# A hybrid decoder layer on one core: four gates of the pooling branch's merge are issued before the state-space tables

## Chip, cores and metric

The kernel runs on one core of a Trainium2 chip. The metric is the device time of one execution in microseconds. Three runs of the kernel before took 1079.84 to 1083.04 us, with a median of 1080.96 us. The engines are named as in the profile: PE (TensorE matmul), PEld (its weight loads), DVE (VectorE), ACT (ScalarE), POOL (GpSimd), SP (SyncE, which issues most DMAs).

## The reference, cut to what matters

The input is 512 tokens of 1024 channels in float32. A token mixer has three branches (sparse attention, pooling, state-space), and a sigmoid gate per channel and branch weighs what each branch sends up to 1024 channels:

```
proj = x @ w_in                       # q, k/v, gates, u_pool, u_ssm, bg in its columns
o_pool = pool_mixer(u_pool)           # 512 x 512
o_ssm = ssm_mixer(u_ssm)              # state-space scan, GELU, GLU
gates = sigmoid(bg)                   # 512 x 3 x 1024
merged = gates[0]*(o_nsa @ w_up_nsa) + gates[1]*(o_pool @ w_up_pool) + gates[2]*(o_ssm @ w_up_ssm)
x = layer_norm(ALPHA*x + merged @ w_out)
```

Then comes a mixture of experts (32 experts, two of them per token) and a second layer norm. The state-space branch has complex diagonal states; it runs as tables of powers, small products within blocks of 8 tokens, and a scan over 64 blocks.

## The kernel before, in words

Everything is kept with channels on the partitions and the 512 tokens along the free dimension. To come near float32 with the faster operand type, each operand is split into a high and a low part, and `mm3` (L68 to L72) makes each product as three matmuls: high by high (L70), low by high (L71), high by low (L72). `proj_fm` projects 128 output channels: `whl` splits the weights (cast on ACT, L113, and a subtraction on POOL, L102, into one of 3 buffers "H"), then 8 x 3 = 24 matmuls of 512 columns run into one of 3 PSUM banks "mm".

`merge` (from L762) works through 8 chunks of 128 channels. For a chunk it makes a gate: such a projection, then `tanh` on ACT (L772) into a tile `th`. Then it makes the up projection of 4 x 3 = 12 matmuls from the branch's output (`oph`/`opl` here) and multiplies both on DVE into `mg` (L780). The first call is the pooling branch's.

Ahead of it, `run` issues in this order: `ssm_u` (the state-space inputs U, L564 to L580), `pool_branch` (window products L746 to L750 with `Bf`, `Bm`, `Bn`; split into `pl`, L278 on ACT and L279 on DVE; a product with the group weights in `ps_o`; output split, L757 on ACT and L758 on DVE), the rotations and tables of the first half of the state-space branch (`ssm_rotations`, `ssm_tables(0)`: long DVE work on `T`, `CA` and `Bs`, then L517 on PE, the transposes L547 and their copies `Bc`), and `ssm_half` for both halves. A half makes X on PE (L601), rotates it on DVE (L606 to L611), scans (L614), rotates back (L322 to L327), makes the output on PE (a block of L633 and L635), and applies GELU quarter by quarter (L639 to L645, into `zz`). After the merge, `ssm_z` transposes `zz` (L654) and splits it into `onh`/`onl` (L659, L660), and `ssm_glu` multiplies by its weights: 48 products.

The order is not written out by hand. A scheduler takes the instructions as they are issued, with priorities, and fixes one sequence for each engine; an engine then works strictly in that sequence and waits where an operand isn't there. Rotations and the first tables are issued with raised priority:

```
        with tc.high_priority(offset=HP):
            self.ssm_rotations()
            tabs = self.ssm_tables(0)
        self.ssm_half(0, U[0], tabs)
        tabs = self.ssm_tables(1)
        self.ssm_half(1, U[1], tabs)
        ...
        for _ in self.merge(1, "w_up_pool", self.oph, self.opl, True):
            pass
```

So in the kernel before, the merge's 288 products have the lowest standing of this stretch, and the scheduler puts them where PE would wait for the state-space work.

Of the kernel before, what the change touches and what calls it, by code (L numbers as in the profile page):

```python
# [8 lines left out]
F32 = mybir.dt.float32  # L9
# [4 lines left out]
AF = mybir.ActivationFunctionType  # L14
# [4 lines left out]
S = 512  # L19
D = 1024  # L20
# [13 lines left out]
C_Q, C_KC, C_VC, C_KS, C_VS, C_KW, C_VW, C_NG, C_POOL, C_SSM, C_BG = (  # L34
    0, 512, 640, 768, 896, 1024, 1152, 1280, 1304, 1816, 2328)
# [8 lines left out]
class Build:  # L44
# [714 lines left out]
                                           op0=OP.mult, op1=OP.subtract)  # L759


    def merge(self, b, wname, oh, ol, first, eng="pool"):  # L762
        nc = self.nc
        p = self.mp
        for dc in range(KD):
            if dc % 4 == 0:
                up = self.load_cols(self.I[wname], D, dc * 128, 512, nk=4)
            if dc % 2 == 0:
                w = self.load_cols(self.I["w_in"], 5400, C_BG + b * D + dc * 128, 256)
            ps = self.proj_fm(w, dc % 2, eng)  # L770
            th = p.tile([128, S], F32, name="th", bufs=2)
            nc.scalar.activation(th, ps, AF.Tanh, scale=0.5)  # L772
            if dc % 2 == 0:
                h, l = self.whl(up[:, :, (dc % 4) * 128:(dc % 4 + 2) * 128], 4, 256, eng=eng)
            js = slice(dc % 2 * 128, dc % 2 * 128 + 128)
            pu = self.bank("mm")
            for k in range(4):
                self.mm3(pu, (h[:, k, js], l[:, k, js]), (oh[:, k], ol[:, k]), k == 0, k == 3)
            if first:
                nc.vector.scalar_tensor_tensor(self.kk(self.mg, dc), th, 1.0, pu, op0=OP.add, op1=OP.mult)  # L780
            else:
                nc.vector.scalar_tensor_tensor(th, th, 1.0, pu, op0=OP.add, op1=OP.mult)
                nc.gpsimd.tensor_tensor(self.kk(self.mg, dc), self.kk(self.mg, dc), th, OP.add)
            yield
# [873 lines left out]
    def run(self):  # L1658
        tc, nc = self.tc, self.nc
# [33 lines left out]
        self.oph, self.opl = pair("P", "oph", "opl")  # L1693
        self.pool_branch(pb)
        spb.close()
        with tc.high_priority(offset=HP):
            self.ssm_rotations()
            tabs = self.ssm_tables(0)
# [3 lines left out]
        self.attn_consts(ggp)  # L1702
        self.mg = (self.slab3("G", "mg", 4), self.slab3("Y", "mg", 4))
        self.mg = [t.bitcast(F32) for t in self.mg]
        for _ in self.merge(1, "w_up_pool", self.oph, self.opl, True):
            pass
        sst.close()
        ssp.close()
        son, onp = self.pool("on")
# [85 lines left out]
```

## Time and profile before

| | |
|---|---|
| runs | 1079.84, 1080.96, 1083.04 us |
| the profiled execution's own time | 1077.99 us |
| its span, first to last instruction | 1076.2 us |
| mean granted clock of TensorE | 0.968 |
| PE busy | 984.6 us (91%), 6189 instructions |
| DVE busy | 600.4 us (56%) |
| ACT busy | 320.2 us (30%) |
| POOL busy | 204.1 us (19%) |

In 40 slices of the span (26.9 us each) the granted clock reads 9985999..., so the third and the fourth slice have a lower one; DMA is busy at 99% in nearly all slices from the 24th on, which is the mixture of experts. A timeline row gives the start and the duration in us, then the engine, the line, the operation and its tiles, and in brackets the engine's idle time before it and what ended it. Matmul durations overlap: the distance from one start to the next is what a matmul costs.

### The profile page before, as it was taken

The page shows a single profiled execution, that of the slowest core. Times are in us where ns is not written, and L with a number is a line of the kernel's source. Part 1 is how long each engine was busy: PE and PEld are TensorE (multiplying, and loading weights), DVE is VectorE, ACT ScalarE, POOL GpSimd, SP SyncE. Part 2 cuts the span into 40 slices and gives each one's busy share as a digit, 9 for nine tenths or more (in the row PEclk, how much of TensorE's full clock was granted, in tenths as well). Part 3 has the DMA queues.
Part 4 walks back from the last instruction along what each step waited for, and adds up shares of the span by engine and source line. Part 5 has one row for each costly group of instructions (what it writes and reads, how often), then busy time and mean ns, then how long its engine had stood idle before and what let it go on. Part 6 is the DMA issues. An engine that isn't in the chain of part 4 may idle for free. (4 is left out here: it accounts for less than half of the span.)

```text
span 1076.2 us, 15925 instructions
## 1 busy us (share of the span) xinstructions
PE 984.6 (91%) x6189; PEld 693.6 (64%) x6189; DVE 600.4 (56%) x1437; ACT 320.2 (30%) x669; POOL 204.1 (19%) x183
## 2 busy tenths in 40 slices
PE   7978988999999999999998999999981999999984
PEld 6966666778777787888885566655541555555542
DVE  7992676474788885244455674444442144444456
ACT  4331222344556665233221211111110211111132
POOL 5520313343202222543322000000000000000004
PEclk9985999999999999999999999999995999999997
DMA  6800451315110202924716999999998999999992
GB/s 194 241 1 8 82 114 46 114 43 177 59 40 1 79 2 69 322 84 170 262 70 254 406 419 417 419 418 418 419 418 343 420 418 418 418 418 418 420 402 83
DMA packets 79566, 256.23 MB, mean 238 GB/s; under 512 B 16544, under 2 KB 43712, under 8 KB 54912
## 3 DMA queue, kind: packets, MB, share of 16 engines
q1 hardware_dynamic: 68064, 245.56, 58.4%
q10 hardware_dynamic: 8368, 2.54, 1.9%
q0 software_dynamic: 3056, 7.08, 1.8%
q8 instruction: 50, 0.82, 0.3%
q14 instruction: 28, 0.23, 0.1%
HBM read 254.40 MB, written 4.69 MB: 241 GB/s over the span
## 5 line engine op out<-in xcount | busy, mean ns | idle before, releaser
L1365 PE MATMUL ps_mm<-w,xq 128*64 128x256 f32 x1296 | 148.8, 381 | 1.7 <-DMA w<-in_moe_w_gate_dram 1.6
L102 POOL TENSOR_TENSOR whl<-w,whl 128x1024 fp32r<-128x1024 f32 (+3 forms) x41 | 95.1, 2328 | 274.4 <-ACT whl L113 236.4
L1365 PEld LDWEIGHTS ps_mm<-w,xq 128*64 128x64 f32 x1296 | 92.7, 137 | 56.5 <-issue 11.7
L70 PE MATMUL ps_mm<-xh,whl 128*128 128x512 f32 x288 | 114.9, 399 | 0.0
L72 PE MATMUL ps_mm<-xh,whl 128*128 128x512 f32 x288 | 114.9, 399 | 0.0
L71 PE MATMUL ps_mm<-xl,whl 128*128 128x512 f32 x288 | 114.3, 397 | 0.0
L1403 DVE TENSOR_TENSOR y<-ps_o,y 64x512 fp32r<-64x512 f32 x60 | 41.3, 689 | 79.3 <-ACT y L1401 73.6
L1345 POOL DMA_INDIRECT xq<-zd,idx x14 | 14.1, 1008 | 368.6 <-PE ps_s L1352 266.5
L1375 DVE SCALAR_TENSOR_TENSOR th<-th,ps_mm 128x256 f32<-128x256 f32 x32 | 13.4, 420 | 111.4 <-ACT th L1374 111.4
L1397 PE MATMUL ps_o<-w,hT 128*64 128x512 f32 x288 | 68.6, 596 | 1.8 <-DMA w<-in_moe_w_down_dram 0.9
L1401 ACT CAST y<-ps_o 64x512 fp32r<-64x512 f32 x60 | 34.8, 580 | 109.2 <-PE ps_o L1397 60.7
L72 PEld LDWEIGHTS ps_mm<-xh,whl 128*128 128x128 f32 x288 | 54.1, 188 | 10.9 <-issue 0.5
L70 PEld LDWEIGHTS ps_mm<-xh,whl 128*128 128x128 f32 x288 | 54.3, 188 | 10.4 <-issue 0.9
L71 PEld LDWEIGHTS ps_mm<-xl,whl 128*128 128x128 f32 x288 | 54.2, 188 | 10.1
L113 ACT CAST whl<-w 128x1024 fp32r<-128x1024 f32 (+3 forms) x56 | 54.7, 988 | 13.4 <-PE ps_mm L72 13.4
L1374 ACT ACTIVATE th<-ps_mm 128x256 f32<-128x256 f32 x32 | 12.3, 384 | 127.3 <-PE ps_mm L1365 127.3
L1365 PE MATMUL ps_mm<-rc,xq 128*64 128x256 f32 x384 | 46.1, 388 | 0.5 <-DMA rc<-in_moe_w_gate_dram 0.5
L1397 PEld LDWEIGHTS ps_o<-w,hT 128*64 128x64 f32 x288 | 21.0, 137 | 36.9 <-issue 31.6
L1365 PE MATMUL ps_mm<-rd,xq 128*64 128x256 f32 x368 | 43.2, 387 | 1.1 <-DMA rd<-in_moe_w_gate_dram 1.1
L1385 ACT COPY hT<-ps_pt 128x256 f32<-128x256 f32 x32 | 11.9, 372 | 94.2 <-PE ps_pt L1384 94.1
L1365 PEld LDWEIGHTS ps_mm<-rc,xq 128*64 128x64 f32 x384 | 28.1, 140 | 17.4 <-issue 3.4
L1352 PE MATMUL ps_s<-ident,xq 128*128 128x128 f32 x112 | 18.0, 306 | 22.8 <-DMA rc<-in_moe_w_up_dram 22.8
(583 smaller groups left out, 2105.9 us busy)
## 6 DMA issues: line engine op xcount, KB each, us to landing
w<-in_moe_w_up_dram SPq DMA_DIRECT2D x43, 1024.0 KB, 20.6
w<-in_moe_w_gate_dram SPq DMA_DIRECT2D x38, 1024.0 KB, 20.6
w<-in_moe_w_down_dram SPq DMA_DIRECT2D x37, 1024.0 KB, 20.1
w<-in_w_in_dram SPq DMA_DIRECT2D x17, 1024.0 KB, 5.1
rc<-in_moe_w_down_dram SPq DMA_DIRECT2D x14, 1024.0 KB, 20.8
rc<-in_moe_w_gate_dram SPq DMA_DIRECT2D x14, 1024.0 KB, 20.6
rd<-in_moe_w_down_dram SPq DMA_DIRECT2D x13, 1024.0 KB, 19.9
rd<-in_moe_w_gate_dram SPq DMA_DIRECT2D x12, 1024.0 KB, 19.9
```

The costliest lines, as they stand in the source:

```text
L70: mm(ps, a[0], b[0], start=start, stop=False)
L71: mm(ps, a[0], b[1], start=False, stop=False)
L72: mm(ps, a[1], b[0], start=False, stop=stop)
L102: (V if eng == "dve" else P)(dst, src, h, OP.subtract)
L113: pin(self.nc.scalar.copy(hv[:, :, c:c + w], src))
L1345: self.nc.gpsimd.indirect_dma_start(xs[:n], None, self.zd[:, :], bass.IndirectOffsetOnAxis(ap=idx, axis=0), bounds_check=S - 1, oob_is_err ...
L1352: self.inorder(self.nc.tensor.transpose(banks[k // 4][:, k % 4 * 128:k % 4 * 128 + n], xs[:n, self.fk(k)], self.ident[:n, :n]))
L1365: self.inorder(nc.tensor.matmul(gu[hh * 64:(hh + 1) * 64, part * 256:(part + 1) * 256], xe[:, k], w[k // 4][:, k % 4, hh * 256:(hh + 1) * ...
L1375: nc.vector.scalar_tensor_tensor(th, th, 1.0, gu[:, 0:256], op0=OP.add, op1=OP.mult)
L1397: self.inorder(nc.tensor.matmul(y[dh][dh * 64:(dh + 1) * 64], hT[:, q, hh * 64:(hh + 1) * 64], wd[f // 2][:, f % 2, dh * 512:(dh + 1) * 51 ...
L1401: nc.scalar.copy(part(yh, dh), y[dh][dh * 64:(dh + 1) * 64])
L1403: nc.vector.tensor_sub(part(yl, dh), y[dh][dh * 64:(dh + 1) * 64], part(yh, dh).bitcast(F32))
```

## The change

Making a gate becomes a function of its own. `run` calls it four times between `pool_branch` and the rotations and tables; the four results wait in two `th` tiles of the pool `mp` and two of a new pool `gt`, and `merge` takes them for its first four chunks. The arithmetic is the same, and so is the number of instructions of each kind.

```
+    def gate(self, b, dc, eng="pool", p=None):
+
+        if dc % 2 == 0:
+            self.wg = self.load_cols(self.I["w_in"], 5400, C_BG + b * D + dc * 128, 256)
+        ps = self.proj_fm(self.wg, dc % 2, eng)
+        th = (p or self.mp).tile([128, S], F32, name="th", bufs=2)
+        self.nc.scalar.activation(th, ps, AF.Tanh, scale=0.5)
+        return th
+
+    def merge(self, b, wname, oh, ol, first, eng="pool", gates=()):
+        nc = self.nc
         for dc in range(KD):
             if dc % 4 == 0:
                 up = self.load_cols(self.I[wname], D, dc * 128, 512, nk=4)
-            if dc % 2 == 0:
-                w = self.load_cols(self.I["w_in"], 5400, C_BG + b * D + dc * 128, 256)
-            ps = self.proj_fm(w, dc % 2, eng)
-            th = p.tile([128, S], F32, name="th", bufs=2)
-            nc.scalar.activation(th, ps, AF.Tanh, scale=0.5)
+            th = gates[dc] if dc < len(gates) else self.gate(b, dc, eng)
...
         self.pool_branch(pb)
         spb.close()
+
+        sgt, gtp = self.pool("gt", side="right")
+        gates = [self.gate(1, dc, p=(self.mp, gtp)[dc // 2]) for dc in range(4)]
         with tc.high_priority(offset=HP):
             self.ssm_rotations()
             tabs = self.ssm_tables(0)
...
-        for _ in self.merge(1, "w_up_pool", self.oph, self.opl, True):
+        for _ in self.merge(1, "w_up_pool", self.oph, self.opl, True, gates=gates):
             pass
+        sgt.close()
```

What the scheduler makes of it stands in the sequence of each engine. First PE where it waits for `pl`, before (`ps_o` is the product of the pool branch with the group weights; `CA` and `bd` are operands of the state-space table product):

```order
L71 MATMUL ps_o<-pl,whl 128x512
L72 MATMUL ps_o<-pl,whl 128x512
L750 MATMUL ps_mm<-Bn,up 128x16
L746 MATMUL ps_mm<-Bf,up 128x16
L747 MATMUL ps_mm<-Bm,up 128x112
L749 MATMUL ps_mm<-Bm,up 128x128
L517 MATMUL ps_s<-CA_1029,bd_375 32x128
L750 MATMUL ps_mm<-Bn,up 128x16
L517 MATMUL ps_s<-CA_1029,bd_375 32x128
L749 MATMUL ps_mm<-Bm,up 128x128
```

The same place in the change, its first rows and then the rows in which the first gate (`ps_mm<-xh,whl` and `ps_mm<-xl,whl`) begins:

```order
L71 MATMUL ps_o<-pl,whl 128x512
L72 MATMUL ps_o<-pl,whl 128x512
L750 MATMUL ps_mm<-Bn,up 128x16
L746 MATMUL ps_mm<-Bf,up 128x16
L747 MATMUL ps_mm<-Bm,up 128x112
L749 MATMUL ps_mm<-Bm,up 128x128
L750 MATMUL ps_mm<-Bn,up 128x16
L749 MATMUL ps_mm<-Bm,up 128x128
```

```order
L70 MATMUL ps_o<-pl,whl 128x512
L750 MATMUL ps_mm<-Bn,up 128x16
L749 MATMUL ps_mm<-Bm,up 128x128
L71 MATMUL ps_o<-pl,whl 128x512
L72 MATMUL ps_o<-pl,whl 128x512
L750 MATMUL ps_mm<-Bn,up 128x16
L70 MATMUL ps_mm<-xh,whl 128x512
L71 MATMUL ps_mm<-xl,whl 128x512
L72 MATMUL ps_mm<-xh,whl 128x512
```

The first L71 stands where it stood; the window products that follow it are no longer interleaved with L517, and the gates follow them. DVE's sequence up to that `pl` is the same as before: it stands behind the last operation on the tables (`Bs`):

```order
L324 TENSOR_TENSOR Bs_1197<-Bs_1197,tt 128x1024
L326 TENSOR_TENSOR tt<-pw,bb_366 128x8x128
L327 TENSOR_TENSOR Bs_1198<-Bs_1198,tt 128x1024
L279 TENSOR_TENSOR pl<-ps_mm,pl 128x512
L758 SCALAR_TENSOR_TENSOR opl<-ps_o,psc,oph 128x512
```

Neither of these rows of DVE has moved. The last place is PE behind the output block of the second half (L633, L635), before:

```order
L635 MATMUL ps_s<-CA_1229,Xq 64x128 x2
L635 MATMUL ps_s<-CA_1230,Xq 64x128 x2
L71 MATMUL ps_mm<-opl,whl 128x512
L72 MATMUL ps_mm<-oph,whl 128x512
L70 MATMUL ps_mm<-oph,whl 128x512
L71 MATMUL ps_mm<-opl,whl 128x512
L72 MATMUL ps_mm<-oph,whl 128x512
```

And in the change (`onh` and `onl` are the two parts of the GLU's input, `zz` what they are transposed from):

```order
L635 MATMUL ps_s<-CA_1356,Xq 64x128 x2
L635 MATMUL ps_s<-CA_1357,Xq 64x128 x2
L70 MATMUL ps_mm<-onh,whl 128x512
L71 MATMUL ps_mm<-onl,whl 128x512
L72 MATMUL ps_mm<-onh,whl 128x512
L70 MATMUL ps_mm<-onh,whl 128x512
L654 MATMUL ps_pt<-ident,zz_167 128x128 x8
L71 MATMUL ps_mm<-onl,whl 128x512
```

The merge's products that stood behind the block have moved ahead of the first half's L601, and the GLU follows the block directly.

## Rows read from the trace of the kernel before

**Rows 1.** Windows by stage: from:to, length, busy of PE, PEld, DVE, ACT, POOL (instructions), clock, DMA share, GB/s

```profile
84.35:105.70 21.35, 21.35 (x82) 14.70 (x83) 3.68 (x7) 4.40 (x8) 0.00 (x0) 0.50 0.02 7
105.70:126.50 20.80, 18.68 (x144) 14.38 (x142) 12.69 (x24) 5.00 (x8) 4.72 (x2) 1.00 0.57 102
...
165.08:180.38 15.30, 11.61 (x106) 8.33 (x105) 14.07 (x22) 3.63 (x5) 7.42 (x3) 1.00 0.21 70
180.38:188.40 8.02, 8.02 (x93) 5.16 (x93) 2.88 (x5) 2.76 (x4) 2.35 (x1) 1.00 0.07 13
...
207.35:222.31 14.96, 13.44 (x65) 10.62 (x64) 11.31 (x17) 7.74 (x15) 6.33 (x3) 1.00 0.23 71
```

**Rows 2.** Timeline of PE around the wait at 84 us

```profile
73.48 0.47 PE L749 MATMUL ps_mm<-Bm,up 128*128 128x128 f32 x2
84.35 0.80 PE L71 MATMUL ps_o<-pl,whl 128*128 128x512 f32 x1 [10.41 <-DVE pl L279]
...
85.37 0.44 PE L750 MATMUL ps_mm<-Bn,up 128*128 128x16 f32 x2
...
87.21 0.64 PE L517 MATMUL ps_s<-CA,bd 128*32 128x128 f32 x2
```

**Rows 3.** Timeline of DVE: the subtraction that PE waits for

```profile
83.61 0.68 DVE L279 TENSOR_TENSOR pl<-ps_mm,pl 128x512 fp32r<-128x512 f32 x1
```

**Rows 4.** Short windows around changes of the clock (last but two column)

```profile
75.00:75.50 0.50, 0.00 (x0) 0.00 (x0) 0.50 (x1) 0.00 (x0) 0.00 (x0) 0.52 0.00 0
...
105.50:106.00 0.50, 0.50 (x3) 0.19 (x1) 0.00 (x0) 0.26 (x1) 0.00 (x0) 0.76 0.00 0
...
836.00:836.50 0.50, 0.50 (x8) 0.29 (x6) 0.00 (x0) 0.00 (x0) 0.00 (x0) 0.81 1.12 475
...
1060.00:1062.00 2.00, 0.53 (x3) 0.11 (x1) 2.00 (x5) 1.14 (x2) 2.00 (x3) 1.00 0.03 8
...
1064.50:1065.00 0.50, 0.00 (x0) 0.00 (x0) 0.50 (x2) 0.00 (x0) 0.50 (x1) 0.89 1.04 375
```

**Rows 5.** Waits of SP's queue, 430 to 800 us: total us, times, longest

```profile
SPq L1450 <- PE ps_mm L72: 40.9, 5, 28.5
```

**Rows 6.** Timeline of PE in a gate at the full clock

```profile
109.29 0.40 PE L70 MATMUL ps_mm<-xh,whl 128*128 128x512 f32 x1
...
113.85 0.39 PE L72 MATMUL ps_mm<-xh,whl 128*128 128x512 f32 x1
```

**Rows 7.** Timeline of PE where it starts again in the mixture of experts

```profile
831.80 1.98 PE L1352 MATMUL ps_s<-ident,xq 128*128 128x128 f32 x8 [22.83 <-DMA rc<-in_moe_w_up_dram]
```

**Rows 8.** Timeline of PE: transposes of zz and the first GLU product

```profile
207.35 1.03 PE L654 MATMUL ps_pt<-ident,zz 128*128 128x128 f32 x8
...
209.19 0.96 PE L70 MATMUL ps_mm<-onh,whl 128*128 128x512 f32 x3 [0.81 <-ACT onh L659]
```

**Rows 9.** Timelines of DVE, POOL and PE in the second half's chain

```profile
166.28 0.42 DVE L606 TENSOR_TENSOR Xq<-T,ps_s 128x256 f32<-128x256 f32 x1 [6.14 <-PE ps_s L601]
...
167.28 1.79 DVE L608 TENSOR_TENSOR Xq<-Xq,tmpx 128x256 f32<-128x256 f32 x1
...
169.98 1.62 DVE L611 TENSOR_TENSOR Xq<-Xq,tmpx 128x256 f32<-128x256 f32 x1
171.52 2.58 DVE L608 TENSOR_TENSOR Xq<-Xq,tmpx 128x256 f32<-128x256 f32 x1
...
166.41 7.42 POOL L102 TENSOR_TENSOR whl<-w,whl 128x1024 fp32r<-128x1024 f32 x3 [17.57 <-ACT whl L113]
...
174.91 0.44 PE L633 MATMUL ps_s<-M,U 128*64 128x128 f32 x4 [2.45 <-DVE tmpx L610]
```

**Rows 10.** Timelines of ACT and DVE: GELU of the second half's quarters

```profile
185.43 0.60 ACT L639 ACTIVATE gt<-ps_s 128x512 f32<-128x512 f32 x1 [1.94 <-PE ps_s L635]
...
188.44 0.69 DVE L645 TENSOR_TENSOR zz<-gt,ps_s 128x512 f32<-128x512 f32 x1
...
189.22 0.60 ACT L639 ACTIVATE gt<-ps_s 128x512 f32<-128x512 f32 x1 [1.28 <-DVE zz L645]
```

More of the change, by code (lines that the diff above doesn't have):

```diff
@@ L759, in pool_branch @@
                                            op0=OP.mult, op1=OP.subtract)
-    def merge(self, b, wname, oh, ol, first, eng="pool"):
+    def gate(self, b, dc, eng="pool", p=None):
[6 more added lines that the diff above has]
+    def merge(self, b, wname, oh, ol, first, eng="pool", gates=()):
         nc = self.nc
-        p = self.mp
         for dc in range(KD):
```

## The prediction

> **What bounds the kernel now.** I read the windows by stage first, then the timelines of PE, DVE, POOL and ACT between 73 and 223 us, then the clock in short windows, and last who SP waits for. The stretch of the change lies between the end of the U projections (73.9 us) and the end of the GLU products (222.31 us). In the windows [rows 1] PE is busy for 11.61 to 21.35 us of each, most of the time, so the stretch is bound by PE's own work, with two flaws at its start. First PE, done at 73.95 us, waits 10.41 us for the subtraction `pl` (L279) [rows 2]: DVE comes to it at 83.61 us, when rotations and tables are through [rows 3]. Then PE works from 84.35 to 105.7 us at a granted clock of 0.50, the lower level (1.2 GHz) [rows 1]. In that time it alternates pool products with L517 products: four pool pairs take 1.84 us, from 85.37 to 87.21 [rows 2]. The clock had fallen between 75.0 and 75.5 us and comes back between 105.5 and 106.0 us [rows 4]. What ends the stretch later is passed on: the MoE's weight loads wait on PE's L72 for 40.9 us in total [rows 5], so I take a shift here one to one into the end.
>
> **What the change moves.** Each engine runs in its written order. The product L71 that waits for `pl` still stands ahead of all gates, and DVE still does `pl` behind the tables. So the 10.4 us of waiting remain; the gates come behind the pool branch, not into the hole. What changes is the order after it. No arithmetic is added: all 8 gates and 8 up projections are still made, 288 products of 512 columns in all, 24 for a gate and 12 for an up projection. I count them in the order, in four pieces. From 84.35 us to the first L635 of half 0 (before: at 126.50 us) there were 59, now 175 (gates 0 to 4, up projections 0 to 3 and 7 products of the next). From there to L601 of half 1 (165.08 us) 109, now 101. From there to L635 of half 1 (180.38 us) 33, now 12. From there to the GLU's end (222.31 us) 87, now none.
>
> **The sum.** A product at the full clock costs 0.228 us: 20 steps from 109.29 to 113.85 us [rows 6].
> - First piece: 116 more products, 116 x 0.228 = +26.4 us. ACT's casts (about 1 us) and POOL's splits (2.4 us) for gates 2 and 3 lie beside gates of 24 x 0.228 = 5.5 us each, so I cost them at nothing; without that cover a gate would wait some 3.4 us.
> - The lower clock ends sooner. After the wait the pool products now follow each other without L517 between: 1.0 us of L71 and L72, the four pairs to 87.21, ten more pairs at the same 0.46 us, then 512-wide products from about 93 us on. In the other place where the clock was low, PE began a dense run at 831.80 us and the clock rose at 836.2 (a mean of 0.81 from 836.0 to 836.5), 4.4 us later [rows 4, 7]. So I expect it back at 93 + 4.4 = 97.4 us instead of 105.7. At half speed that saves 8.3 / 2 = -4.15 us. Bounds: nothing if it comes back no sooner, and -8.5 if it already rises 4.4 us after 84.35.
> - Second piece: 8 fewer, -1.8 us. The waits in it come from the tables of half 1, whose place has not changed.
> - Third piece: 15.30 us [rows 1], set by DVE's chain from L606 to L324, not by PE: 0. PE only loses cover: 21 products (4.8 us) go, and eight transposes of `zz` (1.03 us, as those at 207.35 [rows 8]) come in. Below, the chain could shrink to 10.6 us: three of its operations took 1.79, 1.62 and 2.58 us where their like take 0.42, beside three splits on POOL that ran from 166.41 for 7.42 us [rows 9]; that is 4.7 us. Splits stand at the same place on ACT and POOL now (of the GLU's and the next weights), so I keep 15.3.
> - Last piece: before, 41.93 us; the 83 products behind the scan's output covered the GELU of the last quarter. Now the path is serial: the L633/L635 block without the 4 products among it, 8.02 - 0.9 = 7.1 us [rows 1]; 0.82 until the last quarter's square starts (188.40 to 189.22) and 3.70 for a quarter's GELU, as the quarter before took from 185.43 to 189.13 [rows 10]; 1.84 from the transposes to the first GLU product (207.35 to 209.19) [rows 8]; and the GLU, 13.12 less 4 products done in the wait (0.9) and 8 transposes (1.03), 11.2. Together 24.65, so -17.3 us.
>
> That is 26.4 - 4.15 - 1.8 - 17.3 = **+3.2 us**: the sooner clock doesn't pay for the lost cover.
>
> Then comes the clock again. In the third piece PE now has little to do: behind L633 (before: at 174.91 us [rows 9]) only five transposes stand until L635 5.5 us later, and more waiting lies ahead of it. The clock fell about 1.1 us after PE stopped at 73.95 us, and 4.4 us after it stopped at 1060.53 [rows 2, 4]. So I expect it low when the block of half 1 begins. If it comes back 4.4 us into the block, as at 836 us, that costs 2.2 us; in the 4.5 us of GELU behind the block it falls once more, and eight transposes and 4.4 us of GLU products at half speed cost 1.0 + 2.2. Together +5.4 us. Bounds: 0 if it stays up, and 7.1 + 3.2 = 10.3 if the whole block runs low. I take the middle case: the block alone held the full clock where it ran before (1.00 from 180.38 to 188.40 [rows 1]), so it should also bring it back.
>
> Forecast: 3.2 + 5.4 = **+8.6 us**. The profiled execution took 1077.99 us, 0.3% under the median of the runs, 1080.96. I put the shift on the median: **1089.6 us**. Differences within 0.3% (3.2 us) can't be told from no change.
>
> [...]
>
> **The rivals.**
> 1. The clock falls and the block doesn't bring it back: 64-row products may weigh too little, as the pool and L517 products did for 20 us. Then the block costs 7.1 instead of 2.2: +13.5, 1094.5 us. Against it is the block's full clock before.
> 2. The clock stays up, because L633, transposes and the GLU's first products break the waits. Then only the lost cover remains: +3.2, 1084.2 us, at the edge of what can be told. The two falls speak against it.
> 3. Not slower: the splits on POOL come when DVE's chain needs nothing from it. The second cast of the three on ACT now waits until the last up projection has read its buffer, which is later than before; from the point where it is behind L324, the chain is 10.6 us, PE waits 4.7 us less and need not lose its clock: 3.2 - 4.7 = -1.5, 1079.5 us. The Trainium skill's SBUF — State Buffer, section Who interferes with whom, has the rule: a DVE operation with two SBUF inputs and a GpSimd operation that reads SBUF exclude each other for a whole instruction. The stretched rows [rows 9] agree. Against: at least one split is free to start with the chain.
> 4. The change does what its words say, and gates fill the 10.4 us. The order excludes it, since PE cannot pass L71.
>
> **How the numbers follow.** Forecast 45%, rival 1 20%, rival 2 17%, rival 3 10%, and 8% for orders of size that I don't see (an earlier rise of the clock by up to 4.35 us more, waits for buffers). The range reaches from rival 3 to just above rival 1, 1079.5 to 1096. Slower by over 0.3%: forecast, rival 1 and a part of rival 2, 0.70. Within: rest of rival 2, most of rival 3, 0.24. Faster: 0.06, if an early clock and a short chain come together.
>
> **What would show it.** Right: PE still waits some 10.4 us on L279 at 84 us; the clock returns near 97 us; the first L635 comes near 148 us; no 512-wide product between L635 of half 1 and the GLU; a granted clock of 0.5 there; GLU's end near 231 us. Wrong: the wait on L279 gone, the clock at 1.00 through the last piece, or the GLU's end below 222 us. Also wrong would be a shift at 222 us that isn't found at the end.

## The result, and the profile after

The changed kernel took 1090.05 us (median of 4 runs, 1089.84 to 1092.5), the kernel before 1080.4 us (median of 4): 1.0091 times, with a 95% interval of 1.0075 to 1.0106. The forecast was 1089.6 us.

The profiled execution took 1090.02 us, 12.03 us more than that of before (1077.99). Its GLU products end at 234.26 us, before at 222.31 us, which is 11.95 us later. What comes behind takes as long as before. The windows from the GLU's end to the end of the span, first of after, then of before:

```profile
234.26:1088.00 853.74, 789.82 (x4944) 537.88 (x4942) 449.10 (x1096) 252.43 (x556) 134.13 (x117) 0.98 0.69 275
```

```profile
222.31:1076.00 853.69, 789.81 (x4944) 538.83 (x4942) 448.71 (x1096) 252.61 (x556) 134.37 (x118) 0.98 0.69 275
```

So the whole loss lies ahead of the GLU's end. Whom PE waits for from 70 to 235 us in the kernel after (us in total, times, longest):

```profile
PE ps_o L71 <- DVE pl L279: 11.4, 1, 11.4
PE ps_s L635 <- DVE Xq L324: 6.4, 1, 6.4
PE ps_mm L70 <- ACT onh L659: 3.7, 1, 3.7
PE ps_pt L547 <- DVE Bs L324: 3.5, 1, 3.5
PE ps_s L635 <- DVE Xq L327: 1.8, 2, 1.5
```

The same waits in the kernel before (70 to 223 us):

```profile
PE ps_pt L547 <- DVE Bs L324: 1.4, 1, 1.4
...
PE ps_mm L70 <- ACT onh L659: 1.0, 2, 0.8
PE ps_s L635 <- DVE Xq L324: 0.9, 2, 0.5
```

The first wait is that of [rows 2], one microsecond longer. The second and the third have grown from 1 us or less: ahead of the L635 block of half 1, where 21 more products stood, and behind it, where 83 stood. The windows by stage, in the columns of [rows 1] (length, busy time of PE, PEld, DVE, ACT, POOL, then the granted clock):

```profile
84.03:95.50 11.47, 11.47 (x44) 10.60 (x45) 2.73 (x5) 2.81 (x5) 0.00 (x0) 0.50 0.01 1
95.50:148.88 53.38, 53.38 (x297) 38.55 (x296) 14.59 (x31) 14.53 (x20) 16.65 (x7) 1.00 0.34 82
148.88:189.31 40.43, 35.49 (x238) 26.45 (x237) 27.93 (x28) 7.70 (x14) 7.73 (x3) 0.96 0.39 81
189.31:204.55 15.24, 7.39 (x94) 5.49 (x93) 14.00 (x22) 3.73 (x5) 7.97 (x3) 0.90 0.23 72
204.55:214.91 10.36, 10.04 (x88) 6.30 (x88) 3.05 (x6) 1.23 (x2) 0.00 (x0) 0.65 0.00 0
214.91:218.63 3.72, 0.01 (x2) 0.00 (x1) 2.17 (x5) 1.76 (x4) 0.00 (x0) 1.00 0.00 0
218.63:234.26 15.63, 15.09 (x57) 12.11 (x57) 10.83 (x18) 6.15 (x12) 2.71 (x1) 0.78 0.02 1
```

The lower clock behind the first wait ends at 95.8 us and no longer at 105.7. In exchange PE is busy for only 7.39 of 15.24 us ahead of the block (before 11.61 of 15.30), the block takes 10.36 us (before 8.02), PE then stands for 3.72 us, and the GLU runs at a mean clock of 0.78. When the clock fell and came back, in windows of one microsecond:

```profile
201.00:202.00 1.00, 0.00 (x0) 0.00 (x0) 1.00 (x1) 0.00 (x0) 0.00 (x0) 0.81 0.00 0
211.00:212.00 1.00, 1.00 (x14) 0.74 (x10) 0.00 (x0) 0.26 (x1) 0.00 (x0) 0.57 0.00 0
218.00:219.00 1.00, 0.37 (x1) 0.26 (x1) 0.89 (x2) 0.58 (x3) 0.00 (x0) 0.85 0.00 0
225.00:226.00 1.00, 1.00 (x5) 0.82 (x4) 0.43 (x2) 0.00 (x0) 0.00 (x0) 0.74 0.00 0
```

**An account for all kernels.** To compare kernels with different orders I cut each profiled execution into windows of half a microsecond. A window's length less PE's busy time is PE's idle time; the busy time multiplied by one less the granted clock is what the clock costs; what is left is work at the full clock. Summed from 59.5 us to the GLU's end (all in us; the last column is from there to the end of the span):

| kernel | own time | GLU's end | PE idle | clock | work | behind |
|---|---|---|---|---|---|---|
| before | 1077.99 | 222.31 | 20.6 | 10.7 | 131.6 | 853.9 |
| four gates (the change) | 1090.02 | 234.26 | 28.7 | 14.2 | 131.8 | 854.0 |
| four gates again | 1095.51 | 234.90 | 28.8 | 15.2 | 131.4 | 858.8 |
| three gates | 1076.86 | 220.91 | 19.8 | 7.0 | 134.7 | 854.2 |
| two gates | 1084.88 | 225.76 | 22.8 | 8.6 | 134.8 | 857.3 |
| one gate | 1093.29 | 233.48 | 24.1 | 18.5 | 131.4 | 858.0 |
| idle products | 1092.37 | 231.30 | 20.7 | 9.9 | 141.2 | 859.4 |
| idle products again | 1089.24 | 230.63 | 19.7 | 8.5 | 142.9 | 856.9 |
| two gates in the wait | 1087.62 | 228.74 | 18.9 | 19.4 | 130.9 | 857.1 |
| pool branch first | 1082.10 | 224.98 | 28.0 | 5.5 | 132.0 | 855.4 |
| pl off DVE | 1071.90 | 214.50 | 14.2 | 8.1 | 132.7 | 855.5 |
| the same, one gate | 1066.99 | 208.71 | 10.8 | 3.3 | 135.1 | 856.3 |
| the same, three gates | 1069.66 | 213.80 | 12.6 | 6.3 | 135.4 | 854.0 |
| the same, four gates | 1082.19 | 226.53 | 22.5 | 10.9 | 133.6 | 853.8 |

From before to the change: idle +8.1, clock +3.5, work +0.2. The clock's part is a sum of opposite terms: 4.8 us less behind the first wait, 1.7 more in the stage before half 1's L601, and 6.6 more from the block of half 1 to the GLU's end. In the two places that lost their cover, from half 1's L601 to the GLU's end, idle time grows by 7.2 us, so there the clock costs nearly as much as the waits. The split has a limit: without the idle products all kernels do the same work, and yet that column reads 130.9 to 135.4, so differences of up to 4 us between two kernels may be the method's.

### The profile page after: what moved, and what is told of

It is laid out like the page before. It is cut to its first block, busy times and chain, and to the rows that moved or that the text cites. A ratio compares the mean times of both kernels' runs of the same rounds, so it can differ in the third digit from the quotient of the medians.

```text
span 1088.3 us, 15926 instructions
## 1 busy us (share of the span) xinstructions
PE 988.4 (91%) x6189; PEld 695.1 (64%) x6189; DVE 599.4 (55%) x1437; ACT 319.9 (29%) x669; POOL 203.5 (19%) x183
## 5 line engine op out<-in xcount | busy, mean ns | idle before, releaser
L71 PE MATMUL ps_mm<-xl,whl 128*128 128x512 f32 x288 | 115.6, 401 | 0.0
L71 PEld LDWEIGHTS ps_mm<-xl,whl 128*128 128x128 f32 x288 | 54.5, 189 | 11.2 <-issue 1.4
L70 PEld LDWEIGHTS ps_mm<-xh,whl 128*128 128x128 f32 x288 | 54.5, 189 | 11.2 <-issue 1.5
L862 ACT ACTIVATE P<-P,mx 128x128 f32<-128x128 f32 (+3 forms) x64 | 35.8, 562 | 6.9 <-DVE mx L860 6.9
```

The source lines that it names most:

```text
L70: mm(ps, a[0], b[0], start=start, stop=False)
L71: mm(ps, a[0], b[1], start=False, stop=False)
L862: nc.scalar.activation(t, t, AF.Exp, scale=-1.0, bias=mx[:, hh, br:br + 1], accum_out=sm[:, hh, br:br + 1])
```

## The experiments

The theory: the change loses because gates that are made early no longer cover half 1's chain and GELU. The rivals: every gate made early costs the same; or the loss is the place of the gates behind the wait on `pl`. Behind each quoted expectation stand the measured median, its ratio to the kernel before measured beside it, and the 95% interval.

### One, two and three gates, and four once more

```
-        gates = [self.gate(1, dc, p=(self.mp, gtp)[dc // 2]) for dc in range(4)]
+        gates = [self.gate(1, dc, p=(self.mp, gtp)[dc // 2]) for dc in range(2)]
```

(and `range(1)`, `range(3)`). Two gates:

> Two gates instead of four are issued ahead of the tables; the other two stay in the merge. Theory (lost cover): the wait on the pl of L279 stays at about 11 us at 84 us, as with four. But 33 products stand again between L601 and L635 of half 1, 4 in the block behind, 11 behind the block. Against the changed kernel that gives back 21 products in the wait before L635 (4.8 us), 11 in the wait for the last quarter's GELU (2.5), and the low clock in the block (3.3) and in the GLU (3.2): -13.8 us, so 1075 to 1080 us, with a granted clock of 1.00 in the block. Rival (what costs is to make gates early, each as much as the next: weight splits and L517 among them): half of the loss of 9.7 us stays, about 1085 us.

Measured: 1084.88 us, 1.0045 (1.0027 to 1.0064). Taken by its time alone this was the rival's number.

> One gate instead of four is issued ahead of the tables. Behind half 1's L601 then stand 84 of the merge's products (33, 4 and 47 behind the L635 block) instead of 120 in the kernel before, 48 with two gates and 12 with four. Theory (cover): 47 products are 10.7 us, more than the 5.5 us of GELU that they cover, so no wait comes at the end, and the lower clock ends sooner as with four gates: 1076 to 1081 us, no slower than before. Rival (each gate that is made early costs about 2.4 us, whatever it leaves behind half 1): about 1082 us.

Measured: 1085.45 us (1080.48 to 1093.29), 1.0051 (1.0026 to 1.0076): slower than before, against the cover theory. The rival had the direction; its 2.4 us over the kernel before lie just below the interval.

> Three gates instead of four are issued ahead of the tables. Behind half 1's L601 the order is that with two gates: 33 products, 4 and 11. Theory (cover): the same time as with two gates, 1084 to 1086 us, and the whole step to the changed kernel (1090) comes with the fourth gate, which takes 36 products away there. Rival (each gate costs the same): 1087 to 1088 us.

Measured: 1080.51 us, 1.0011 (0.9998 to 1.0025): no slower than before. The rival is wrong; the time does not grow with the number of gates, and the step of some 9.5 us to the changed kernel comes with the fourth, as the cover theory said (by the ratios, 0.8% or 8.6 us). Its number for three gates was too high by 4 us, and cover alone doesn't tell why one and two gates are slower than three.

> The changed kernel once more, unaltered, beside the two others of this call on one chip, to see how far its loss repeats: 1088 to 1092 us, by either theory.

Measured: 1093.89 us, 1.0109 (1.0074 to 1.0144). The loss repeats; the median lies 2 us above the expected range.

Whom PE waits for with three gates, in the lines that answer to those of the change:

```profile
PE ps_o L71 <- DVE pl L279: 10.5, 1, 10.5
...
PE ps_mm L71 <- DVE onl L660: 2.1, 1, 2.1
PE ps_mm L70 <- ACT onh L659: 1.6, 2, 1.3
...
PE ps_s L635 <- DVE Xq L327: 1.1, 1, 1.1
```

The 6.4 us ahead of the block are gone, and the block (8.16 us) runs at the full clock:

```profile
193.14:201.30 8.16, 8.16 (x94) 5.30 (x94) 2.03 (x5) 2.76 (x4) 2.35 (x1) 1.00 0.18 49
```

Why are one and two gates slower than three, with the same or more cover? With one gate the scheduler mixes its products one by one with pairs of L517, right behind the pool products. The clock stayed at 0.50 until 113 us, though PE had no idle time:

```profile
84.03:96.00 11.97, 11.97 (x49) 9.94 (x49) 3.23 (x5) 2.81 (x5) 0.00 (x0) 0.50 0.01 1
96.00:113.00 17.00, 17.00 (x41) 6.94 (x41) 1.40 (x3) 1.38 (x2) 0.00 (x0) 0.50 0.00 0
```

With two or more gates products of 512 columns come in runs ahead of the L517 pairs, and the clock is back at 95 to 97 us. With two gates the profile has 3.0 us more idle time than with three: waits for POOL's splits (2.1 us, with three gates 0.6) and for CA (1.4) lead the difference. The profile of one gate was its slowest run (1093.29 us, with a mean granted clock of 0.955; its fastest, 1080.48 us, had 0.970). The run at the median had 0.966, about that of the kernel before, so what its median pays stays open.

### Idle products that hold the clock

```
+        po = self.bank("o")
+        for i in range(10):
+            nc.tensor.matmul(po, self.ident, self.kk(self.mg, 6), start=(i == 0), stop=(i == 9))
         sgt.close()
```

> The changed kernel with ten added products of 512 columns in float32 (identity by a finished chunk of mg) whose result nobody reads; the scheduler puts six into the wait before L635 of half 1, one into the L635 block and three behind it. They do no useful work and leave all waits on DVE and ACT. Theory (part of the loss is the clock that falls in these waits): clock near 1.00 through the block and the GLU, 3.3 and 3.2 us back, 0.8 us lost for the one in the block: -5.7 us, about 1084.4 us (1083 to 1086). Rival (the waits alone cost, and the clock comes back by itself too soon to matter): 1090 to 1092 us.

Measured: 1090.84 us, 1.0087 (1.0057 to 1.0117), the rival's number. The same kernel again:

> The kernel with ten idle products once more, with more runs, since its first four left open what they bring. Theory (the clock's part of the loss reaches the end): its GLU ended 3.0 us sooner than the changed kernel's, so a ratio to the kernel before of 1.006 to 1.0075 where the changed kernel has 1.009 to 1.011. Rival (short falls of the clock later in the run take it back): a ratio of 1.009 or more.

Measured: 1088.95 us, 1.0085 (1.0067 to 1.0103). The block and the GLU in the first of them:

```profile
204.90:214.41 9.51, 9.51 (x91) 5.34 (x91) 2.90 (x6) 1.23 (x2) 0.00 (x0) 0.82 0.00 0
214.41:218.53 4.12, 3.66 (x17) 1.94 (x15) 2.56 (x5) 1.95 (x4) 0.00 (x0) 1.00 0.00 0
218.53:231.30 12.77, 12.44 (x56) 9.87 (x57) 9.97 (x18) 6.13 (x12) 2.48 (x1) 1.00 0.02 1
```

The GLU ran at the full clock and took 12.77 us where it took 15.63, and it ended 3.0 us sooner (231.30 against 234.26). The block began at the full clock, but the clock fell at 205.9 us, one microsecond into the block, and was back at 209.3. From the block's start to the GLU's end the clock costs 1.7 us by the account (6.6 in the change); the end gains only 3.0, as one idle product stands in the block and three behind it. At the end of the program even that isn't found: both profiles have a further fall of 7.5 us some 137 us behind the GLU's end (the change's second profile has it too, its first not), and the second ratio lies between the two expectations. What holding the clock is worth in total stays open: the edit held it only in part and paid for it with products of its own. The waits on DVE and ACT are still there; PE now does work in them that nobody needs.

### Two gates ahead of the pool branch

```
+        sgt, gtp = self.pool("gt", side="right")
+        gates = [self.gate(1, dc, p=(self.mp, gtp)[dc // 2]) for dc in range(2)]
         self.pool_branch(pb)
         spb.close()
-
-        sgt, gtp = self.pool("gt", side="right")
-        gates = [self.gate(1, dc, p=(self.mp, gtp)[dc // 2]) for dc in range(4)]
```

> Two gates are issued ahead of the pooling branch instead of behind it, so that 48 products of 512 columns stand on PE ahead of the L71 that waits for pl. Theory (the change put its gates behind the wait, and that is why it could not pay): 48 x 0.228 = 10.9 us fill the wait of 10.4 us, the clock does not fall at 75 us, and the pool branch's products and L517 run at 1.00 instead of 0.50 (10.7 us back). Lost against the kernel before is cover at the end (11 products behind the block of half 1 instead of 83), 1 to 4 us. About 1062 us (1059 to 1067). Rival 1 (the products fill the wait, but those of the pool branch and L517 don't hold the clock): about 1073 us. Rival 2 (DVE's chain from L517 to L635 of half 0 sets the time there, not PE): no faster than 1070 us, with new waits of PE on DVE before 126 us.

Measured: 1086.72 us, 1.005 (1.0029 to 1.007): the theory's number is missed by 25 us. Stretches around the wait, PE and clock:

```profile
79.80:84.77 4.97, 4.96 (x42) 4.53 (x40) 4.87 (x4) 2.71 (x4) 3.17 (x1) 1.00 0.02 3
84.77:87.82 3.05, 0.00 (x0) 0.00 (x0) 3.02 (x4) 0.00 (x0) 0.06 (x1) 0.90 0.00 0
87.82:104.00 16.18, 16.18 (x67) 10.89 (x68) 3.19 (x6) 2.85 (x6) 0.00 (x0) 0.50 0.00 0
```

The products do fill the wait: 3.05 us of it are left. But these 3 us were enough for the clock to fall, and the pool products with L517 then ran at 0.50 until 107.6 us, as in the kernel before. And those 3 us the gates made themselves. POOL's two splits for their weights, at 76.17 us (2.71 long) and at 81.60 (3.23), ran beside DVE's tables:

```profile
76.66 3.44 DVE L509 SCALAR_TENSOR_TENSOR CA<-CA,tt 128x1152 f32<-128x1152 f32 x1
...
82.65 3.26 DVE L326 TENSOR_TENSOR tt<-pw,bb 128x1024 f32<-128x1024 f32 x1
...
87.08 1.28 DVE L279 TENSOR_TENSOR pl<-ps_mm,pl 128x512 fp32r<-128x512 f32 x2
```

L509 takes 1.36 us and L326 1.23 in the kernel before; so `pl` came 3.5 us later than there. Later there were new waits: 2.7 us for Xq (at 137 us), 3.6 for CA (at 160), 2.5 for POOL's splits. Rival 1 is missed too; rival 2 has only its bound of time, for the new waits on DVE come later than it said. The wait was filled, and nothing gained.

### The pool branch at the tables' priority

```
-        self.pool_branch(pb)
+        with tc.high_priority(offset=HP):
+            self.pool_branch(pb)
```

> The kernel before with the whole pooling branch issued at the tables' raised priority; all gates stay in the merge. On DVE the subtraction pl then comes ahead of the tables, and PE does the pool branch among the transposes of the U inputs. The cover behind half 1 is that of the kernel before. Theory (the wait on pl and the low clock behind it are the one flaw worth mending, 10.4 + 10.7 us): about 1060 us (1058 to 1066). Rival (pl and opl, eight operations of 0.7 us, push the tables back on DVE, and PE runs out of products before L517 and the transposes of Bs): a new wait of 5 to 10 us between 75 and 100 us, the clock low again, 1070 to 1077 us.

Measured: 1083.8 us, 1.0035 (1.0019 to 1.0051). The edit did not do what I expected of it: PE's products moved ahead, DVE's `pl` did not; it still follows the last table operation (L327 at 82.45 us). So neither the theory nor its rival was put to the test. PE and DVE:

```profile
84.34 0.79 PE L71 MATMUL ps_o<-pl,whl 128*128 128x512 f32 x1 [18.67 <-DVE pl L279]
```

```profile
83.60 1.28 DVE L279 TENSOR_TENSOR pl<-ps_mm,pl 128x512 fp32r<-128x512 f32 x2
```

The wait grew to 18.67 us, while the clock came back after 4.2 us of work (at 88.5 us). In the account +7.4 us of idle time and -5.2 of clock.

### pl off DVE, without and with gates

```
-            self.split2(ps, h, l)
+            nc.scalar.copy(h, ps)
+            f = self.mp.tile([128, S], F32, name="th", bufs=2)
+            nc.scalar.copy(f, ps)
+            nc.gpsimd.tensor_tensor(l, f, h.bitcast(F32), OP.subtract)
...
-            nc.vector.scalar_tensor_tensor(self.opl[:, g], po, psc[:, g:g + 1], self.oph[:, g].bitcast(F32),
-                                           op0=OP.mult, op1=OP.subtract)
+            f = self.mp.tile([128, S], F32, name="th", bufs=2)
+            nc.scalar.activation(f, po, AF.Copy, scale=psc[:, g:g + 1])
+            nc.gpsimd.tensor_tensor(self.opl[:, g], f, self.oph[:, g].bitcast(F32), OP.subtract)
```

> The kernel before with the low parts pl and opl of the pooling branch made by a second copy on ACT and a subtraction on POOL, instead of a subtraction on DVE; no gate is moved, and 83 products cover the end as in the kernel before. Theory (the 10.4 us of waiting and the low clock behind it are the flaw): L71 no longer waits for DVE; PE waits at most 4 us for CA at L517; 10 to 18 us less, 1062 to 1070 us. Rival (POOL's eight subtractions of about 1.2 us stretch DVE's tables, so that L517 and the transposes of Bs wait instead): 1075 to 1082 us, with DVE's operations on CA and Bs at over 2 us where they took 1.2 to 1.4.

Measured: 1071.9 us, 0.9943 (0.9923 to 0.9962), about 7 us less. The theory has the direction, not the size. Two of PE's waits (70 to 235 us):

```profile
PE ps_s L517 <- DVE CA L509: 6.4, 2, 3.6
...
PE ps_o L71 <- POOL pl L757: 0.9, 1, 0.9
```

The 10.4 us are down to 0.9, but L517 now waits for CA, 3.6 us at the longest, and the clock is low from 80.7 to 94.3 us. The rival has a part in it: two of DVE's operations on CA took 2.31 and 2.30 us beside POOL's subtractions, where the others took 1.36.

```profile
76.67 2.31 DVE L508 TENSOR_TENSOR tt<-C,pw 128x1152 f32<-128x1152 f32 x1
79.01 2.30 DVE L509 SCALAR_TENSOR_TENSOR CA<-CA,tt 128x1152 f32<-128x1152 f32 x1
```

> As the kernel with pl off DVE, and with one gate issued behind the pooling branch and ahead of the tables; L517 comes behind the pool products, and 83 of the merge's products still stand behind the L635 block of half 1. Theory: 24 products of 512 columns (5.5 us) fill what is left of the wait and hold the clock, 15 to 21 us less than before: 1059 to 1066 us. Rival (as for the kernel with pl off DVE alone): 1075 us or more.

Measured: 1073.12 us (1066.67 to 1077.59), 0.994 (0.9909 to 0.9972). Its profiled execution (1066.99 us) has no fall of the clock before 115 us and only 10.8 us of idle time; its median is no better than without a gate and lies between the two expectations.

The same with three gates. "The kernel before" in the quoted text is the next one below, with four gates and `pl` off DVE:

> As the kernel before in this call, with three gates ahead: 48 products behind half 1's L601 (33, 4 and 11). Theory (cover; the step comes with the fourth gate): 1068 to 1074 us, as with one gate, and 8 us or more under four gates. Rival (each gate made early costs 2.4 us): about 1078 us.

Measured: 1072.32 us, 0.993 (0.9898 to 0.9962), in the theory's range.

> The changed kernel (four gates behind the pooling branch, ahead of the tables) with pl and opl off DVE, so that the wait on L279 is gone and the gates do fill what was a wait. Behind half 1's L601 stand 12 products, as in the changed kernel. Theory (the changed kernel loses by its lost cover, and the wait at 84 us is a flaw of its own beside it): 8 to 12 us over the kernel with pl off DVE and one gate, 1080 to 1085 us, with an idle PE of 5 to 7 us ahead of L635 of half 1 and 3 to 4 us behind the block. Rival (the changed kernel loses because its gates stand behind that wait; with it gone they pay): 1074 us or less.

Measured: 1081.09 us, 1.0002 (0.9987 to 1.0016), 8.8 us over three gates, in the theory's range. This settles the last rival: with the wait at 84 us gone, the fourth gate costs what it cost with the wait. Its waits at half 1 are those of the changed kernel:

```profile
PE ps_s L635 <- DVE Xq L324: 6.4, 1, 6.4
...
PE ps_mm L70 <- ACT onh L659: 3.9, 1, 3.9
PE ps_pt L547 <- DVE Bs L324: 3.5, 1, 3.5
```

The wait at 84 us and the lost cover are two flaws beside each other. The change left the first and made the second. Of all kernels here those with `pl` off DVE and up to three gates are the best: they beat the kernel before by 0.6 to 0.7%, and the change by 1.5%.

## Why the prediction was right

1. **The wait stays.** Predicted 10.4 us, measured 11.38; `pl` came at 83.29 us (before 83.61), and PE stood ready 1.3 us sooner. Rival 4 (the gates fill it) did not happen.
2. **First piece.** Predicted +26.4 - 4.15 = +22.25; from 84.03 to 148.88 us are 64.85 us against 42.15 before, +22.70. The clock came back at 95.8 us, not 97.4, 2.4 us behind the first gate product at 93.44. That gained 0.8 us more. A term that I did not have stands against it: 13 pairs of L517 stand one by one among products of a gate, and pair and product take 0.76 us (113.26 to 114.02 below), where a product alone takes 0.228. By the account the +22.70 are work +29.6, clock -4.8 and idle -2.1: 3.2 us more work than the 26.4 of the products, and two waits of PE (0.5 and 1.6 us before 122 us) that are gone and that the sum did not have. That these nearly cancel is luck.

```profile
113.26 0.41 PE L517 MATMUL ps_s<-CA,bd 128*32 128x128 f32 x2
113.59 0.49 PE L71 MATMUL ps_mm<-xl,whl 128*128 128x512 f32 x1
114.02 0.41 PE L517 MATMUL ps_s<-CA,bd 128*32 128x128 f32 x2
```

3. **Second piece: the step that failed.** "The waits in it come from the tables of half 1, whose place has not changed" gave -1.8 us. Before, the piece was this:

```profile
126.50:165.08 38.58, 35.76 (x245) 27.02 (x246) 25.90 (x28) 9.18 (x15) 8.70 (x3) 1.00 0.39 86
```

Now it took 40.43 us, +1.85: by the account work -2.0, idle +2.1 and clock +1.7. The tables' place had not changed, but where POOL's splits fell beside DVE's operations had. Before, they stretched two of them (their like take 1.35 and 1.21), by 3.8 us together:

```profile
138.12 3.52 DVE L507 TENSOR_TENSOR CA<-C,pw 128x1152 f32<-128x1152 f32 x1
...
147.10 2.81 DVE L324 TENSOR_TENSOR Bs<-Bs,tt 128x1024 f32<-128x1024 f32 x1
```

In the change one split begins at 149.01 us (2.75 long) and two more at 168.18. Beside them L327 took 2.74 us (its like 0.68), L643 2.25 (0.43 at 214.29) and L323 3.41 (1.21), 6.1 us more together:

```profile
168.18 4.98 POOL L102 TENSOR_TENSOR whl<-w,whl 128x1024 fp32r<-128x1024 f32 x2 [16.42 <-ACT whl L113]
```

```profile
149.56 2.74 DVE L327 TENSOR_TENSOR Xq<-Xq,tmpx 128x504 f32<-128x504 f32 x1
...
168.66 2.25 DVE L643 TENSOR_SCALAR gt<-gt 128x512 f32<-128x512 f32 x1 [0.28 <-ACT gt L642]
170.84 3.41 DVE L323 TENSOR_TENSOR tt<-pw,bb 128x1024 f32<-128x1024 f32 x1
```

So PE waited 1.46 us for Xq (L327) and 3.48 for Bs, where it had waited 1.4 for CA and 1.4 for Bs, and the clock fell once, for 4 us (the 0.96 in that stage). The change's second profile has the same two waits and one such fall, behind the other wait. I had looked for this mechanism in the third piece alone. It is read from the rows; no run here takes the splits away. The operations that were stretched, here and in the experiments, read two tiles of SBUF (L323, L324, L326, L327, L507 to L509, L608, L611) or are L643; L606, L607, L609 and L610, which read PSUM, took 0.41 to 0.42 us beside the splits that began at 190.64 us. The rule of the Trainium skill (SBUF — State Buffer, Who interferes with whom) says this of operations with two SBUF inputs, and the trace agrees; L643, with one, lies outside that sentence.
4. **Third piece.** Predicted 15.3 us, set by DVE's chain and not by PE; measured 15.24, with PE waiting 6.4 us. Rival 3 (a shorter chain) did not come: three of its operations were again stretched beside POOL's splits, to 1.81, 1.60 and 2.49 us.
5. **Last piece.** Predicted 24.65 + 5.4 = 30.05 us, measured 29.71. The parts differ, and that they cancel is luck. The clock fell at 201 us, ahead of the block (so rival 2 is out), and came back about 7 us into it (in the window from 211 to 212), not 4.4; it fell again at 218 and was back at 225 us. The block took 10.36 us, where 7.1 + 2.2 = 9.3 were predicted and rival 1 has 14.2; the GLU took 15.63, predicted 11.2 + 3.2 = 14.4. The serial path was shorter in turn: behind the block PE stood for 3.72 us, where I had 4.5 us of GELU and 1.84 to the first GLU product. The first GLU products do not need the last quarter: they take the half whose eight transposes ended at 198.11 us. What they waited for is a cast that stands behind the last GELU in ACT's sequence:

```profile
217.95 0.63 ACT L659 CAST onh<-ps_pt 128x256 fp32r<-128x256 f32 x2
```

ACT had been idle for 14.77 us before the GELU began at 211.74 us. Whether the cast could have run there no run shows; if so, part of this wait is a matter of ACT's order.
6. **The sum.** Predicted +8.6 us. Profile against profile it was +11.95 at the GLU's end, and the second piece (3.65) makes the difference; between the medians it was +9.65. The profile of before was one of its kernel's faster runs, so the near hit of the median (0.45 us) rests in part on that, which is luck.

That the lost cover is the cause is shown by the step from three to four gates, twice and alike (9.5 and 8.8 us); that the clock has a part in it is shown only up to the GLU's end.

## What to carry to other kernels

Low-priority matmuls are a store of cover: ask of each one moved forward which later wait it was going to hide, and read its new place from the order. Here three gates moved cost nothing and the fourth some 9 us, so count what is left behind the last long chain. More cover is no safe order by itself: one and two gates left as much or more of it and were slower than three. A wait on another engine's queue is cured at that queue (here by taking `pl` off DVE), not by issuing more work behind it.

## What was not expected

- **When the clock came back.** After a wait, 17 us without any idle time, with pairs of L517 (32 rows) one by one among products of 512 columns, stayed at 0.50 (one gate). In the change the clock was back 2.4 us into products of 512 columns in a row. In the kernel with the pool branch first, 4.2 us of pool products and transposes brought it back. Ahead of a wait the clock stayed at 1.00 through 5 us of the same pool products (79.8 to 84.77 us, two gates in the wait). What decides is not shown.
- **Falls that come and go.** Code that no edit touched has short falls of the clock in some executions. The same stretch behind the GLU in the change and in its second profile:

```profile
372.50:380.50 8.00, 8.00 (x43) 6.06 (x43) 6.37 (x23) 4.59 (x15) 0.00 (x0) 1.00 0.17 66
```

```profile
372.50:380.50 8.00, 8.00 (x29) 6.06 (x27) 4.23 (x16) 3.22 (x11) 0.00 (x0) 0.57 0.24 92
```

PE is busy in all of it both times; 43 of its instructions fall into it at a clock of 1.00, 29 at 0.57. Such falls make most of the differences in the last column of the account, up to 5.6 us, so one profile of this kernel is good for no more than some 3 us.
